# Adaptive-norm modulation in four column groups, token rows loaded between its units

## The chip, the cores and the metric

One Trainium2 chip, one core of it. The metric is the device time of one execution in microseconds (us); the kernel before takes 2986.76 us (median of three runs, 2984.95 to 2987.01). One execution was also recorded by the hardware profiler. The engines are named as in the profile: PE is the matrix engine, PEld its weight loads, DVE the vector engine, ACT the scalar engine, POOL the general engine, SP the engine whose queue issues nearly all DMAs.

## The reference, cut to what matters

Two blocks of two transformer layers, on 512 tokens of width 1024 and 256 context tokens. The first block modulates its norms by a condition vector:

```
def adaln(cond, w, b):
    m = jnp.matmul(jax.nn.silu(cond), w) + b
    return jnp.split(m, 3, axis=-1)
...
for layer in range(DEPTH):
    shift, scale, gate = adaln(c, w_ada[layer], b_ada[layer])
    c_shift, c_scale, c_gate = adaln(c_ctx, w_ada[layer], b_ada[layer])
    h = modulated_norm(x, norm_g[layer], shift[:, None], scale[:, None])
    h_ctx = modulated_norm(x_ctx, norm_g[layer], c_shift, c_scale)
    p = jnp.matmul(h, w_in[layer])
    ...
    x = x + gate[:, None] * jnp.matmul(y, w_out[layer])
```

`w_ada[layer]` is 1024 x 3072. Only two rows (c and c_ctx) are multiplied with it, so the work is loading 12.6 MB a layer and streaming it through PE. Layer 0 mixes tokens by global attention (GQA) and by a long convolution (the hyena branch), whose filters come from a small network and are used in the frequency domain. All outputs are f32.

## The kernel before, in words

Ordinary products run as three matmuls on f32 numbers split into a high and a low part (`mm3`, L81 to L83; splits at L54 and L55). The modulation does not: `ada` (L141 to L183) multiplies in f32 itself. It goes over chunks of 512 of the 3072 columns. A chunk has four units; a unit loads 512 KB of weights into a tile `st` (L151; the tag `st` has four buffers, which every other weight uses too) and does two f32 matmuls (L160) whose stationary operand is two columns of the condition (`c2`) and whose moving operand is 128 x 512 weights. Eight matmuls add up in rows 0 and 1 of one PSUM tile. ACT copies these two rows (L164). For chunks 0 to 3 (shift and scale) four small transposes turn them into columns, DVE adds the bias (L171), and after chunk 3 the per-channel factors modA and modB are made (L181, L182). For chunks 4 and 5 (gate) the two rows go to DRAM, `grow` (L175). `gate_tile` (L185) later loads a gate row spread over all partitions (L188), loads the bias spread in the same way (L193) and adds it on POOL (L195).

The stages of layer 0 are written as generators that yield a cost after each piece of work. `merge` and `mix` (L1681 to L1698) take two of them and always advance the one that has used the smaller share of its declared total. A list scheduler behind the program then reorders each engine's instructions within their dependencies. The stages, with the times at which they ran:

- A, 0 to 265 us: the filter network and filter transforms (`hy_mlp`, `hy_kernels`) merged with `inputs()`. `inputs()` does the 16 units of layer 0's chunks 0 to 3, then loads the 6 blocks of token rows (2 of context, 4 of x; L202, tag `oa`), normalises them (`rms`, L206 to L219: squares on ACT, factors and products on DVE), transposes and modulates them (`mod_T`, L222 to L241) and projects them for the hyena branch.
- 265 to 340 us: the projections of the attention.
- C, about 340 to 448 us: attention merged with gates 4 to 7 and the 16 units of layer 1's chunks 0 to 3.
- D, 448 to 535 us: gates 0 to 3, then layer 0's gate chunks 4 and 5 (8 units), merged with the context's convolution.
- E, 535 to 662 us: the long convolution of x merged with the context's output and layer 1's chunks 4 and 5 (8 units).

Of the kernel before, what the change touches and what calls it, by code (L numbers as in the profile page):

```python
# [15 lines left out]
P = 128  # L16
# [11 lines left out]
class Net:  # L28
# [109 lines left out]
        self.split(V[:, :, 0], V[:, :, 1], s)  # L138


    def ada(self, l, chunks, exact=True, tag='o'):  # L141

        nc, I = self.nc, self.I
        nr = 2 if exact else 4
        self.exact[l] = exact
        for c in chunks:
            ps = self.ps(tag)
            for kk in range(4):
                if exact:
                    w = self.t('st', [P, 1024])  # L150
                    nc.sync.dma_start(w, I[f'ada{l}'][c * 4 + kk])  # L151
                    w = [w]
                else:
                    st, w = self.t('st', [P, 1024]), [self.t('a', [P, 1024], R) for _ in range(2)]
                    nc.sync.dma_start(st, I[f'ada{l}'][c * 4 + kk])
                    self.split(w[0], w[1], st)
                cc = self.c2 if exact else self.c4
                for j in range(2):
                    for x, v in enumerate(w):
                        nc.tensor.matmul(ps[:nr], cc[:, 2 * kk + j], v[:, j * 512:(j + 1) * 512],  # L160
                                         start=kk + j + x == 0, stop=2 * kk + j == 7 and x == len(w) - 1)
                yield 1.7 if exact else .85
            row = self.t('v2', [P, 512])
            nc.scalar.activation(row[:nr], ps[:nr], AF.Copy)  # L164
            if c < 4:
                pT = self.ps('pt')
                for b in range(4):
                    self.tr(pT[:, b * nr:(b + 1) * nr], row[:nr, b * P:(b + 1) * P], nr)
                pv = pT[:, :4 * nr].rearrange("p (m j) -> p m j", j=nr)
                d = self.adaT[l][:, c * 4:c * 4 + 4]  # L170
                nc.vector.tensor_tensor(d, pv[:, :, 0:2], self.adabT[l][:, c * 4:c * 4 + 4], op=OP.add)  # L171
                if not exact:
                    nc.vector.tensor_tensor(d, pv[:, :, 2:4], d, op=OP.add)
            else:
                nc.sync.dma_start(self.grow[l][0:nr, (c - 4) * 512:(c - 3) * 512], row[:nr])  # L175
            if c == 3:
                self.mod[l] = []
                for j in range(2):
                    a = self.cn.tile([P, 8], F, name=f"modA{l}_{j}")
                    b = self.cn.tile([P, 8], F, name=f"modB{l}_{j}")  # L180
                    nc.vector.scalar_tensor_tensor(a, self.adaT[l][:, 8:16, j], 1.0, self.ngc[l], op0=OP.add, op1=OP.mult)  # L181
                    nc.vector.tensor_copy(b, self.adaT[l][:, 0:8, j])  # L182
                    self.mod[l].append((a, b))  # L183

    def gate_tile(self, l, j):  # L185
        nc = self.nc
# [328 lines left out]
    def hy_taps(self, o, hf, ni, w3, C):  # L515
# [287 lines left out]
    def first_consts(self):  # L803
        nc, I = self.nc, self.I
        self.ones = self.cn.tile([P, P], F, name="ones")
        nc.gpsimd.memset(self.ones, 1.0)
        self.c2 = self.cn.tile([P, 8, 2], F, name="c2")
        cc = self.const('cT', I['cT'])
        nc.scalar.activation(self.c2, cc, AF.Tanh, scale=0.5)
        nc.vector.tensor_scalar(self.c2, self.c2, 0.5, 0.5, op0=OP.mult, op1=OP.add)  # L810
        nc.vector.tensor_tensor(self.c2, self.c2, cc, op=OP.mult)
        self.mod, self.exact = [None, None], [None, None]
        self.grow = [self.scratch(f"grow{l}", [4, 1024]) for l in range(2)]
        self.c4 = self.cn.tile([P, 8, 4], R, name="c4")
        self.split(self.c4[:, :, 0:2], self.c4[:, :, 2:4], self.c2)
        self.adaT = [self.cn.tile([P, 16, 2], F, name=f"adaT{l}") for l in range(2)]

    def more_consts(self):
# [6 lines left out]
    def layer0(self, each):  # L825
# [4 lines left out]
        Y = []  # L830

        def inputs():
            ada = self.ada(0, range(4), True)
            for _ in range(3):
                yield next(ada)
            self.more_consts()
            yield from ada
            xc, xs = self.load_rows(I['ctx'], 2, 'oa'), self.load_rows(I['x'], 4, 'oa')
            self.rms(xc)
            self.rms(xs)  # L840
            hc, hx = self.ctx_T(), self.new_T()
            H.extend((hc, hx))
            yield 1
# [20 lines left out]
        def att():  # L864
# [4 lines left out]
            for g in range(2):  # L869
                K = C['K'][g]  # L870
                for i in range(4):
# [6 lines left out]
        self.merge(att(), 82, self.chain(self.gates('w0', 18, st, (4, 5, 6, 7)), self.ada(1, range(4), True, 'mm')), 58)  # L878
        self.merge(self.chain(self.gates('w0', 18, st, (0, 1, 2, 3)), self.ada(0, (4, 5), True)), 31,
                   self.hyena(1, yc[2:]), 13)  # L880

        def ctx_out():
            y = self.y_split(yc, 256)
            xc = self.load_rows(I['ctx'], 2)
            yield from self.out_proj('wout0', y, 2, xc, self.gate_tile(0, 1), lambda i: None)
            del y
            self.hc1 = self.ctx_h(xc)
            yield 2
            yield from self.ada(1, range(4, 6), True)
# [1046 lines left out]
    def build(self, stage="all"):  # L1936
        tc, nc, I = self.tc, self.nc, self.I
        with ExitStack() as top:
# [14 lines left out]
            if first:  # L1953
                self.first_consts()
                hx = None
                if stage == 'l1':
                    self.xscr = I['x']
                    self.more_consts()
                    self.run(self.ada(1, range(6), False))
# [66 lines left out]
def constants():  # L2026
# [21 lines left out]
    for n in (512, 256):  # L2048
# [6 lines left out]
        for ix in tok[n]:  # L2055
            zf.append(z[ix])
            dec.append(d[ix])
    C['hyz'] = np.concatenate(zf, 0).T.astype(f32)
    C['hydec'] = np.stack(dec, 0).astype(f32)
    row0 = np.ones((P, 1), f32)  # L2060
    row0[0] = 0
# [154 lines left out]
```

## Time and profile before

| | |
|---|---|
| median of three runs | 2986.76 us |
| the profiled execution, its own time | 2990.1 us |
| its span, first to last instruction | 2988.3 us |
| PE busy | 2819.3 us, 94% |
| DVE busy | 1973.2 us, 66% |
| ACT busy | 1347.9 us, 45% |
| POOL busy | 266.8 us, 9% |
| mean granted PE clock | 0.98 |
| PE busy in the first 80 us | 61.6 us |

Busy time is a sum over stages with different limits, so each stage has to be read by itself: how much of it PE worked, and where PE did not, what it waited for. An f32 matmul shows as two records of PE, each with its own weight load. The name `oa`, `st` or `grow` in a row is that of the tile, and L160 is the line of the program that issued it.

### The profile page before, as it was taken

The numbers are of one execution on the slowest core, as the hardware profiler recorded it, in microseconds if no ns is written. First come the engines' busy times: TensorE is split into PE (matmuls) and PEld (weight loads), VectorE is DVE, ScalarE is ACT, GpSimd is POOL, SyncE is SP. The second block draws the span as 40 slices with busy tenths as digits, with TensorE's granted clock in tenths as the row PEclk, the third lists the DMA queues.
The fourth block names the chain that finished last, engine by engine and source line by source line (L and its number), as shares of the span: only waits on it lengthen the run. The fifth ranks groups of instructions, "written<-read, shape, count | busy, mean of one in ns | idle before, by whom it ended". The sixth has DMA issues, their size and how long they took to land.

```text
span 2988.3 us, 40380 instructions
## 1 busy us (share of the span) xinstructions
PE 2819.3 (94%) x14904; PEld 2286.7 (77%) x14904; DVE 1973.2 (66%) x4419; ACT 1347.9 (45%) x2763; POOL 266.8 (9%) x310
## 2 busy tenths in 40 slices
PE   7999899889899999999999899999999999899998
PEld 3788757557888778777788788888787778788886
DVE  5767867986787756876755843436787664954435
ACT  6543445343345644565543522324565552633222
POOL 0212101101211310100110000000000011000000
PEclk8999999989999999999999999999999999999999
DMA  6433132653213423221124132233231124223231
GB/s 225 136 123 97 36 106 85 218 183 104 76 54 112 123 84 99 95 70 61 55 85 148 65 120 90 95 106 123 66 98 58 57 71 148 85 85 112 93 98 64
DMA packets 117645, 299.76 MB, mean 100 GB/s; under 512 B 21471, under 2 KB 48031, under 8 KB 117448
## 3 DMA queue, kind: packets, MB, share of 16 engines
q1 hardware_dynamic: 117448, 297.19, 30.3%
q8 instruction: 117, 1.92, 0.3%
q14 instruction: 80, 0.66, 0.1%
HBM read 273.54 MB, written 27.54 MB: 101 GB/s over the span
## 4 chain that ended last, share of the span: by engine, by line
PE 60%; DVE 8%; ACT 3%; issue 1%; DMA 0%; POOL 0%; ACTq 0%; DVEq 0%
PE mm L81 15%; PE mm L82 15%; PE mm L83 15%; PE pt L86 4%; PE o L120 2%; PE o L121 1%; PE o L1026 1%; DVE u L55 1%; PE o L1437 1%; PE S L1632 1%; DVE a L1141 1%; PE S L1633 1%; PE o L1492 1%; DVE a L1137 0%; PE S L1402 0%
## 5 line engine op out<-in xcount | busy, mean ns | idle before, releaser
L81 PE MATMUL mm<-a,u 128*128 128x512 f32 (+1 forms) x1596 | 595.8, 375 | 6.5 <-ACT a L54 2.4
L82 PE MATMUL mm<-a,u 128*128 128x512 f32 (+1 forms) x1596 | 593.1, 372 | 0.0
L83 PE MATMUL mm<-a,u 128*128 128x512 f32 (+1 forms) x1596 | 588.9, 370 | 0.4 <-DVE u L55 0.4
L54 ACT ACTIVATE u<-st 128x1024 fp32r<-128x1024 f32 x352 | 368.7, 1051 | 409.6 <-PE mm L83 355.1
L55 DVE TENSOR_TENSOR u<-st,u 128x1024 fp32r<-128x1024 f32 x340 | 427.9, 1259 | 130.6 <-ACT u L54 124.2
L81 PE MATMUL mm<-u,a 128*128 128x512 f32 (+1 forms) x1280 | 459.7, 360 | 10.8 <-DVE v L259 3.7
L82 PE MATMUL mm<-u,a 128*128 128x512 f32 (+1 forms) x1280 | 458.1, 358 | 4.6 <-DVE u L55 4.6
L83 PE MATMUL mm<-u,a 128*128 128x512 f32 (+1 forms) x1280 | 458.3, 358 | 0.0
L81 PEld LDWEIGHTS mm<-a,u 128*128 128x128 f32 x1596 | 302.2, 190 | 57.6 <-ACT a L54 4.3
L83 PEld LDWEIGHTS mm<-a,u 128*128 128x128 f32 x1596 | 302.6, 190 | 47.3 <-DVE u L55 1.0
L82 PEld LDWEIGHTS mm<-a,u 128*128 128x128 f32 x1596 | 303.0, 190 | 44.4 <-issue 1.5
L81 PEld LDWEIGHTS mm<-u,a 128*128 128x128 f32 x1280 | 243.0, 190 | 48.0 <-ACT u L54 3.7
L82 PEld LDWEIGHTS mm<-u,a 128*128 128x128 f32 x1280 | 243.4, 190 | 39.6 <-DVE u L55 6.8
L83 PEld LDWEIGHTS mm<-u,a 128*128 128x128 f32 x1280 | 243.2, 190 | 34.6 <-DVE a L58 0.6
L86 PE MATMUL pt<-c_ident,e 128*128 128x128 f32 x1132 | 191.1, 279 | 37.6 <-DVE e L273 9.4
L55 DVE TENSOR_TENSOR va<-pt,va 128x512 fp32r<-128x512 f32 (+2 forms) x252 | 163.6, 668 | 72.4 <-ACT va L54 71.3
L54 ACT ACTIVATE va<-pt 128x512 fp32r<-128x512 f32 (+2 forms) x252 | 140.7, 582 | 155.8 <-PE pt L86 153.0
L1206 DVE SCALAR_TENSOR_TENSOR a<-a,mm 128x512 f32<-128x512 f32 x96 | 65.7, 684 | 213.1 <-PE mm L83 213.0
L86 PEld LDWEIGHTS pt<-c_ident,e 128*128 128x128 f32 x1132 | 135.7, 141 | 82.4 <-issue 34.8
L1891 DVE TENSOR_TENSOR v<-v 128x512 f32<-128x512 f32 x64 | 44.3, 692 | 157.4 <-ACT v L1890 157.4
L1890 ACT ACTIVATE v<-mm 128x512 f32<-128x512 f32 x60 | 36.0, 600 | 200.3 <-PE mm L83 200.3
L82 PE MATMUL S<-u,a 128*128 128x256 f32 x312 | 90.1, 289 | 1.4 <-DVE u L55 1.4
(425 smaller groups left out, 4948.1 us busy)
## 6 DMA issues: line engine op xcount, KB each, us to landing
st<-in_up SPq DMA_DIRECT2D x64, 512.0 KB
st<-in_dn SPq DMA_DIRECT2D x64, 512.0 KB
st<-in_w SPq DMA_DIRECT2D x52, 512.0 KB
st<-in_ada SPq DMA_DIRECT2D x48, 512.0 KB
st<-in_gate SPq DMA_DIRECT2D x48, 512.0 KB
st<-in_win SPq DMA_DIRECT2D x42, 512.0 KB
st<-in_wout SPq DMA_DIRECT2D x24, 512.0 KB
st<-in_br SPq DMA_DIRECT2D x16, 512.0 KB
```

What stands on the lines that cost most here:

```text
L54: nc.scalar.activation(hi, src, AF.Copy)
L55: (eng or nc.vector).tensor_tensor(lo, src, hi.bitcast(F), op=OP.subtract)
L81: mm(ps, ah, bh, start=first, stop=False)
L82: mm(ps, ah, bl, start=False, stop=False)
L83: mm(ps, al, bh, start=False, stop=last)
L86: self.nc.tensor.transpose(dst, src, self.ident[:n, :n])
L120: nc.tensor.matmul(o, v, ph[:nk], start=first and bi == 0, stop=False)
L121: nc.tensor.matmul(o, v, pl[:nk], start=False, stop=last and bi == len(blocks) - 1)
L1026: nc.tensor.matmul(o[s * 64:(s + 1) * 64, i * P:(i + 1) * P], v[:, hd * 64:(hd + 1) * 64], pe[:, b * P:(b + 1) * P], start=b == 0, stop=b ...
L1206: self.nc.vector.scalar_tensor_tensor(xx, xx, alpha, ps, op0=OP.mult, op1=OP.add, **kw)
L1890: nc.scalar.activation(r, ps, AF.Relu)
L1891: nc.vector.tensor_tensor(sq, r, r, op=OP.mult)
```

## The change

- `ada`: the stationary operand is 32 columns wide, two of the condition and zeros behind them (`cw`), and the eight matmuls of a chunk go to four groups of 32 output partitions in turn, so neighbours write different columns of the array. Each group adds up two of the eight. ACT copies all 128 rows. For chunks 0 to 3 four f32 matmuls with a constant (`asel`) sum the groups and turn them into columns in one step. For chunks 4 and 5 the bias row is loaded into row 2 of the copy (2 KB), one f32 matmul with `asel` sums groups and bias, ACT copies two rows, and these go to `grow`.
- `gate_tile` is one load; the bias loads and the POOL adds are gone.
- The declared costs: a unit yields 0.5 where it yielded 1.7, and 3.0 inside `inputs()`.
- `inputs()` loads the token rows behind unit 3 of 16 and normalises them behind units 4 and 5; the declared total of that stream goes from 135 to 156.
- `hy_taps` takes its tiles from the tag `oa` in one case, (o, hf) = (0, 1), and from `u` in the others.

```diff
-    def ada(self, l, chunks, exact=True, tag='o'):
+    def ada(self, l, chunks, tag='o', pace=0.5):
...
                 for j in range(2):
-                    for x, v in enumerate(w):
-                        nc.tensor.matmul(ps[:nr], cc[:, 2 * kk + j], v[:, j * 512:(j + 1) * 512],
-                                         start=kk + j + x == 0, stop=2 * kk + j == 7 and x == len(w) - 1)
-                yield 1.7 if exact else .85
+                    k = 2 * kk + j
+                    g = slice(32 * (k % 4), 32 * (k % 4) + 32)
+                    nc.tensor.matmul(ps[g], self.cw[:, 2 * k:2 * k + 32], w[:, j * 512:(j + 1) * 512], start=k < 4, stop=k >= 4)
+                yield pace
             row = self.t('v2', [P, 512])
-            nc.scalar.activation(row[:nr], ps[:nr], AF.Copy)
+            nc.scalar.activation(row, ps, AF.Copy)
             if c < 4:
                 pT = self.ps('pt')
                 for b in range(4):
-                    self.tr(pT[:, b * nr:(b + 1) * nr], row[:nr, b * P:(b + 1) * P], nr)
+                    nc.tensor.matmul(pT[:, 2 * b:2 * b + 2], row[:, b * P:(b + 1) * P], self.asel[:, 0:2],
+                                     start=True, stop=True)
...
             else:
-                nc.sync.dma_start(self.grow[l][0:nr, (c - 4) * 512:(c - 3) * 512], row[:nr])
+                nc.sync.dma_start(row[2:3], I[f'adab{l}'][0:1, c * 512:(c + 1) * 512])
+                pg = self.ps('pt')
+                nc.tensor.matmul(pg[:2], self.asel[:, 2:4], row, start=True, stop=True)
+                gr = self.t('v2', [P, 512])
+                nc.scalar.activation(gr[:2], pg[:2], AF.Copy)
+                nc.sync.dma_start(self.grow[l][:, (c - 4) * 512:(c - 3) * 512], gr[:2])
...
         g = self.t('a', [P, 1024])
-        nc.sync.dma_start(g, rowb(self.grow[l], 1024, j * 1024))
-        low = [] if self.exact[l] else [(self.grow[l], (j + 2) * 1024)]
-        for src, off in low + [(self.I[f'adab{l}'], 2048)]:
-            for c in range(2):
-                b = self.t('v2', [P, 512])
-                nc.sync.dma_start(b, rowb(src, 512, off + c * 512))
-                sl = slice(c * 512, (c + 1) * 512)
-                nc.gpsimd.tensor_tensor(g[:, sl], g[:, sl], b, op=OP.add)
+        self.nc.sync.dma_start(g, rowb(self.grow[l], 1024, j * 1024))
         return g
...
-        if ni == 0 and hf == 0:
+        if ni == 0 and (o, hf) == (0, 1):
             E = [self.t('oa', [P, 2, 2, 256], R) for _ in range(nb)]
...
-            ada = self.ada(0, range(4), True)
+            ada = self.ada(0, range(4), pace=3.0)
             for _ in range(3):
                 yield next(ada)
             self.more_consts()
+            xc, xs = self.load_rows(I['ctx'], 2, 'oa'), self.load_rows(I['x'], 4, 'oa')
+            for _ in range(1):
+                yield next(ada)
+            self.rms(xc)
+            yield next(ada)
+            self.rms(xs)
             yield from ada
-            xc, xs = self.load_rows(I['ctx'], 2, 'oa'), self.load_rows(I['x'], 4, 'oa')
-            self.rms(xc)
-            self.rms(xs)
...
-        self.merge(self.chain(self.hy_mlp(), self.hy_kernels(1), self.hy_kernels(0)), 115, inputs(), 135)
+        self.merge(self.chain(self.hy_mlp(), self.hy_kernels(1), self.hy_kernels(0)), 115, inputs(), 156)
```

What this does to the order of instructions, at three places.

SP's queue in stage A, before: `in_ada` is the modulation's weights, `in_dft` and `in_hyw` belong to the filters, `in_ctx` and `in_x` are the token rows. These are the last units of chunks 0 to 3.

```order
L202 DMA oa_372<-in_ctx 128x1024
L506 DMA st_292<-in_dft 128x1024
L151 DMA st_307<-in_ada 128x1024
L151 DMA st_311<-in_ada 128x1024
L494 DMA st_315<-in_hyw 64x1024 x2
L151 DMA st_328<-in_ada 128x1024
L151 DMA st_332<-in_ada 128x1024
L202 DMA oa_374<-in_ctx 128x1024
L202 DMA oa_376<-in_x 128x1024
```

The same queue in the change, right behind the constants, at the fourth unit:

```order
L44 DMA c_hyc<-in_hyc 128x48
L194 DMA oa_174<-in_ctx 128x1024
L194 DMA oa_176<-in_ctx 128x1024
L194 DMA oa_178<-in_x 128x1024
L194 DMA oa_180<-in_x 128x1024
L194 DMA oa_182<-in_x 128x1024
L194 DMA oa_184<-in_x 128x1024
L152 DMA st_186<-in_ada 128x1024
```

All six row blocks (3.1 MB) now stand ahead of units 4 to 16; before, five of the six stood behind the last unit.

PE in stage C, before, where layer 1's first chunk starts (`mm_4130` is the modulation's PSUM tile, S and o the attention's):

```order
L83 MATMUL mm_3970<-a_455,u_3938 128x256
L160 MATMUL mm_4130<-st_4131,c_71 2x512
L404 MATMUL S_3813<-a_2313,a_2670 128x512
L405 MATMUL S_3813<-a_2313,a_2670 128x512
L404 MATMUL S_3818<-a_2313,a_2670 128x512
L405 MATMUL S_3818<-a_2313,a_2670 128x512
L160 MATMUL mm_4130<-st_4131,c_71 2x512
```

The same place in the change:

```order
L83 MATMUL mm_3968<-a_552,u_3936 128x256
L156 MATMUL mm_4128<-st_4129,cw 32x512
L385 MATMUL S_3805<-a_2313,a_2668 128x256 x4
L156 MATMUL mm_4128<-st_4129,cw 32x512
L156 MATMUL mm_4128<-st_4133,cw 32x512 x2
L156 MATMUL mm_4128<-st_4137,cw 32x512
L396 MATMUL S_3811<-a_2311,a_2668 128x512
L397 MATMUL S_3811<-a_2311,a_2668 128x512
```

The modulation's matmuls were mostly alone between others and now stand in longer runs.

SP at the end of stage E in the change (L170 loads a bias row into the copied rows, L175 stores the gate row, `in_wout` is the output weight); before, L175 stood there twice with no load ahead of it:

```order
L152 DMA st_5962<-in_ada 128x1024
L170 DMA v_1187_5867<-in_adab 1x512
L1174 DMA st_6138<-in_wout 128x1024
L1174 DMA st_6143<-in_wout 128x1024
L1174 DMA st_6148<-in_wout 128x1024
L175 DMA grow_81<-v_1189_5872 2x512
L170 DMA v_1215_5966<-in_adab 1x512
```

And PE there (L172 sums groups and bias, the S matmuls belong to the long convolution):

```order
L156 MATMUL o_5875<-st_5962,cw 32x512 x2
L172 MATMUL pt_5870<-v_1187_5867,c_asel 2x512
L172 MATMUL pt_5969<-v_1215_5966,c_asel 2x512
L81 MATMUL S_5945<-a_5562,a_5722 128x512
L82 MATMUL S_5945<-a_5563,a_5722 128x512
L83 MATMUL S_5945<-a_5562,a_5723 128x512
```

The second L172 has to wait for a load that stands behind the store of the first one's result.

## Rows read from the trace of the kernel before

**Rows 1.** The page: busy time, share of the span and instructions of each engine
```profile
PE 2819.3 (94%) x14904; PEld 2286.7 (77%) x14904; DVE 1973.2 (66%) x4419; ACT 1347.9 (45%) x2763; POOL 266.8 (9%) x310
```

**Rows 2.** Busy time by stretch; columns in the first line
```profile
core 0: us, PE busy (x) PEld busy (x) DVE busy (x) ACT busy (x) POOL busy (x), PEclk, DMA share, GB/s
0.00:54.00 54.00, 47.03 (x152) 16.17 (x152) 26.30 (x59) 24.80 (x44) 3.23 (x8) 0.97 0.80 259
54.00:80.00 26.00, 14.60 (x61) 10.86 (x60) 21.22 (x62) 24.85 (x55) 0.82 (x1) 0.67 0.32 110
80.00:265.00 185.00, 171.93 (x1079) 154.63 (x1079) 129.94 (x189) 87.63 (x139) 39.59 (x26) 0.97 0.39 123
...
387.00:448.00 61.00, 61.00 (x231) 25.88 (x230) 38.67 (x93) 29.88 (x79) 0.73 (x1) 1.00 0.42 129
448.00:535.00 87.00, 83.28 (x432) 59.81 (x432) 70.50 (x139) 43.44 (x99) 10.29 (x8) 1.00 0.28 89
535.00:662.00 127.00, 101.66 (x389) 65.62 (x388) 116.64 (x169) 50.59 (x79) 11.16 (x6) 0.90 0.59 204
```

**Rows 3.** PE timeline, 53 to 61 us: start, us, work [idle before, releaser]
```profile
53.49 0.64 PE L541 MATMUL S<-a,v 128*128 128x256 f32 x4
60.85 2.20 PE L86 MATMUL pt<-c_ident,oa 128*128 128x128 f32 x8 [6.72 <-DVE oa L219]
```

**Rows 4.** Line L214 (rms): count, duration in ns min/median/max, first and last start
```profile
L214 ACT ACTIVATE v<-oa x12: 612/613/614, 51.6 to 61.8; 128x512 f32<-128x512 f32 x12
L214 ACT ACTIVATION_READ_ACCUMULATOR v<-oa x12: 184/186/187, 52.1 to 62.3; 128x1 f32 x12
```

**Rows 5.** Line L160, the modulation's records on PE, same columns
```profile
L160 PE MATMUL o<-st,c x128: 589/592/1057, 8.1 to 652.7; 128*2 128x512 f32 x128
...
L160 PE MATMUL mm<-st,c x64: 591/592/593, 387.6 to 447.4; 128*2 128x512 f32 x64
```

**Rows 6.** PE timeline around a run and around a single f32 matmul
```profile
35.59 3.60 PE L160 MATMUL o<-st,c 128*2 128x512 f32 x8
...
387.30 0.28 PE L82 MATMUL mm<-a,u 128*128 128x256 f32 x1
387.42 0.28 PE L83 MATMUL mm<-a,u 128*128 128x256 f32 x1
387.63 1.02 PE L160 MATMUL mm<-st,c 128*2 128x512 f32 x2
388.58 0.50 PE L404 MATMUL S<-a,a 128*128 128x512 f32 x1
388.92 0.40 PE L405 MATMUL S<-a,a 128*128 128x512 f32 x1
389.15 0.40 PE L404 MATMUL S<-a,a 128*128 128x512 f32 x1
```

**Rows 7.** PE timeline: the four small transposes, and 32 matmuls with 64 moving columns
```profile
18.05 0.41 PE L86 MATMUL pt<-c_ident,v 2*128 2x2 f32 x4
...
1235.96 3.76 PE L1492 MATMUL o<-a,st 128*128 128x64 f32 x32 [0.31 <-issue]
```

**Rows 8.** SP timeline: the modulation's loads, the token rows, a small load
```profile
0.74 0.40 SPq L44 DMA_DIRECT2D c_cT<-in_cT  x1
...
17.15 13.32 SPq L151 DMA_DIRECT2D st<-in_ada  x6
...
45.02 1.93 SPq L202 DMA_DIRECT2D oa<-in_x  x4
```

**Rows 9.** ACT: the small load's reader, and the copies of line L164
```profile
2.37 0.21 ACT L809 ACTIVATE c<-c_cT 128x16 f32<-128x16 f32 x1 [0.35 <-DMA c_cT<-in_cT]
...
L164 ACT ACTIVATE v<-o x8: 573/587/591, 17.2 to 653.3; 2x512 f32<-2x512 f32 x8
```

**Rows 10.** PE timeline at the end of stage E
```profile
636.86 3.60 PE L160 MATMUL o<-st,c 128*2 128x512 f32 x8
...
647.47 0.40 PE L81 MATMUL S<-a,a 128*128 128x512 f32 x1
```

**Rows 11.** Line L195, the gate's bias adds on POOL
```profile
L195 POOL TENSOR_TENSOR a<-a,v x6: 1267/1484/2341, 574.6 to 1085.1; 128x512 f32<-128x512 f32 x6
```

More of the change, by code (lines that the diff above doesn't have):

```diff
@@ L138, in vsplit @@
         self.split(V[:, :, 0], V[:, :, 1], s)
-    def ada(self, l, chunks, exact=True, tag='o'):
+    def ada(self, l, chunks, tag='o', pace=0.5):
         nc, I = self.nc, self.I
-        nr = 2 if exact else 4
-        self.exact[l] = exact
         for c in chunks:
@@ L148, in ada @@
             for kk in range(4):
[L149 to L157, printed above, removed]
+                w = self.t('st', [P, 1024])
+                nc.sync.dma_start(w, I[f'ada{l}'][c * 4 + kk])
                 for j in range(2):
-                    for x, v in enumerate(w):
-                        nc.tensor.matmul(ps[:nr], cc[:, 2 * kk + j], v[:, j * 512:(j + 1) * 512],
-                                         start=kk + j + x == 0, stop=2 * kk + j == 7 and x == len(w) - 1)
-                yield 1.7 if exact else .85
+                    k = 2 * kk + j
+                    g = slice(32 * (k % 4), 32 * (k % 4) + 32)
+                    nc.tensor.matmul(ps[g], self.cw[:, 2 * k:2 * k + 32], w[:, j * 512:(j + 1) * 512], start=k < 4, stop=k >= 4)
+                yield pace
             row = self.t('v2', [P, 512])
-            nc.scalar.activation(row[:nr], ps[:nr], AF.Copy)
+            nc.scalar.activation(row, ps, AF.Copy)
             if c < 4:
@@ L167, in ada @@
                 for b in range(4):
[L168 to L169 removed]
+                    nc.tensor.matmul(pT[:, 2 * b:2 * b + 2], row[:, b * P:(b + 1) * P], self.asel[:, 0:2],
+                                     start=True, stop=True)
                 d = self.adaT[l][:, c * 4:c * 4 + 4]
[L171 to L175 removed]
+                nc.vector.tensor_tensor(d, pT[:, :8].rearrange("p (m j) -> p m j", j=2),
+                                        self.adabT[l][:, c * 4:c * 4 + 4], op=OP.add)
+            else:
+                nc.sync.dma_start(row[2:3], I[f'adab{l}'][0:1, c * 512:(c + 1) * 512])
[4 more added lines that the diff above has]
+                nc.sync.dma_start(self.grow[l][:, (c - 4) * 512:(c - 3) * 512], gr[:2])
             if c == 3:
@@ L806, in first_consts @@
         nc.gpsimd.memset(self.ones, 1.0)
-        self.c2 = self.cn.tile([P, 8, 2], F, name="c2")
+        self.cw = self.cn.tile([P, 46], F, name="cw")
+        nc.gpsimd.memset(self.cw, 0.0)
+        c2 = self.cw[:, :16].rearrange("p (k j) -> p k j", j=2)
         cc = self.const('cT', I['cT'])
[L809 to L815, printed above, removed]
+        self.asel = self.const('asel', I['asel'])
+        nc.scalar.activation(c2, cc, AF.Tanh, scale=0.5)
+        nc.vector.tensor_scalar(c2, c2, 0.5, 0.5, op0=OP.mult, op1=OP.add)
+        nc.vector.tensor_tensor(c2, c2, cc, op=OP.mult)
+        self.mod = [None, None]
+        self.grow = [self.scratch(f"grow{l}", [2, 1024]) for l in range(2)]
         self.adaT = [self.cn.tile([P, 16, 2], F, name=f"adaT{l}") for l in range(2)]
@@ L877, in layer0 @@
         self.run(self.gqa_proj('w0', ((hc, 2, 1, True), (hx, 4, 0, True)), gain, C))
-        self.merge(att(), 82, self.chain(self.gates('w0', 18, st, (4, 5, 6, 7)), self.ada(1, range(4), True, 'mm')), 58)
-        self.merge(self.chain(self.gates('w0', 18, st, (0, 1, 2, 3)), self.ada(0, (4, 5), True)), 31,
+        self.merge(att(), 82, self.chain(self.gates('w0', 18, st, (4, 5, 6, 7)), self.ada(1, range(4), 'mm')), 58)
+        self.merge(self.chain(self.gates('w0', 18, st, (0, 1, 2, 3)), self.ada(0, (4, 5))), 31,
                    self.hyena(1, yc[2:]), 13)
@@ L888, in ctx_out @@
             yield 2
-            yield from self.ada(1, range(4, 6), True)
+            yield from self.ada(1, range(4, 6))
         self.merge(self.hyena(0, yx[2:]), 49, ctx_out(), 48)
@@ L1958, in build @@
                     self.more_consts()
-                    self.run(self.ada(1, range(6), False))
+                    self.run(self.ada(1, range(6)))
                     self.hc1 = self.ctx_h(self.load_rows(I['ctx0'], 2))
@@ L2058, in constants @@
     C['hyz'] = np.concatenate(zf, 0).T.astype(f32)
+    sel = np.zeros((P, 4), f32)
+    for j in range(2):
+        sel[j::32, j] = 1
+        sel[j::32, 2 + j] = 1
+    sel[2, 2:] = 1
+    C['asel'] = sel
     C['hydec'] = np.stack(dec, 0).astype(f32)
```

1 line of the change is left out of this document (removed).

## The prediction
> **What bounds the kernel now.** I read the page's engine table first: PE works 94% of the span, nothing else over 66% [rows 1]. So time comes from PE, either as work taken off it or as holes filled. Then the busy times by stretch, for the stages that the change touches [rows 2]. The reader is to see four different stages. In the first 54 us PE works 47.03, and the DMA engines 0.80 of the time at 259 GB/s. From 54 to 80 us PE works only 14.60 of 26. Stage C has PE at 61.00 of 61 us and stage D at 83.28 of 87: PE sets their lengths. In stage E DVE works 116.64 of 127 us and PE 101.66: there DVE leads. Third, PE's timeline at the hole behind 54 us [rows 3]: PE stands 6.72 us until DVE has normalised the first token rows, so `rms` is last there. Line L214 shows why [rows 4]: its 12 squares, 0.613 + 0.186 us each, 9.6 us in all, start at 51.6 us, when the modulation is done. Last, the modulation's own records [rows 5, 6].
>
> **What a modulation matmul costs.** There are 128 + 64 records [rows 5] for 96 matmuls, two each, 64 matmuls and 128 records outside stage C. A run of 8 records takes 3.60 us, the last one 0.59: (3.60 - 0.59)/7 = 0.43 us apart [rows 6], 0.86 us a matmul. Around a single one the starts are farther apart: 0.21 us into it where its neighbours are 0.12 apart, 0.95 us for itself, and 0.34 behind it where 0.23 is usual [rows 6]. That is 0.09 + 0.09 + 0.11, about 0.28 us for every run of them, whatever its length.
>
> The order counts 26 runs in stage C before and 15 after (lengths 1, 4, 3, 1, 1, 2, 1, 4, 3, 2, 2, 2, 2, 1, 3), 7 before and 5 after in D (8, 1, 3, 2, 2).
>
> **How far column groups overlap** is what the sum hangs on, and no row of this trace has matmuls in different column groups side by side. Bounds: nothing overlaps (0.86 each, runs alone get fewer), or four always run as one. I take the value between. A matmul is two records into the same columns, so the second must follow the first, 0.43 us later, as now. In every row read here PE starts records in program order. So, if groups overlap, the second record of one can run beside the first of the next, and a run of n takes (n + 1) x 0.43 + 0.28 us.
>
> The Trainium skill (TensorEngine Tiling (Array Packing), Theoretical Speedup) gives up to four times for 32 columns and says that tiles work independently (Key Properties). By it the sum below would be that of the first rival. The page TensorE: Matmul & The Clock Gate, Part 3, has three column groups measured at 2.38 times, and says that matmuls start and end in program order; the latter, applied to two records a matmul, leads to my middle value. No row here shows either.
>
> **The change, part by part.**
>
> *Stage A.* Rows and `rms` leave the tail. First, what it can win: the hole of 6.72 us [rows 3], plus the waits that ACT's 9.6 us of squares [rows 4] put into the modulating chain; PE has 11.4 us of holes from 54 to 80 [rows 2]. Second, what it can lose: the rows' 3.1 MB now stand ahead of 13 of 16 units on SP. Up to 54 us 14.0 MB come in (259 x 54); at the same share-to-rate ratio full use would be 259/0.80 = 324 GB/s, 43 us for the same bytes. So the rows fit into capacity that was idle, and the last unit stays near 51 us. Were they not to fit, 3.1 MB at 259 GB/s is 12 us, of which the hole's 6.72 are paid back: a loss of 5. PE's own modulation there shortens as well, but shorter than its weights' arrival it can't get. I take -8, the hole and little more, since the rest of the chain (ACT and DVE 24.85 and 21.22 of 26 us busy [rows 2]) stays. Bounds -16 and +5. The `oa`/`u` exchange and `cw` have one answer, nothing: buffers, with PE's other work beside them.
>
> *Stage C.* 32 matmuls. Before: 64 records x 0.43 + 26 x 0.28 = 34.8 us. After: (32 + 15) x 0.43 + 15 x 0.28 = 24.4. That is -10.4, all on the path, as PE is full. Added: the four sums of L163 are f32 too, 8 records with full-width weights; 32 matmuls that are short on the moving side take 3.76 us, 0.12 each [rows 7], so 0.94 a chunk against 0.41 for the four transposes: +0.5 x 4 chunks. Stage C: -8.3. Bounds: -15.6 (15 groups of 0.86 + 0.28 = 17.1) and -1.0 (64 x 0.43 + 15 x 0.28 = 31.7).
>
> *Stage D.* 16 matmuls: 32 x 0.43 + 7 x 0.28 = 15.7 before, 21 x 0.43 + 5 x 0.28 = 10.4 after, -5.3. Two L172 are added at 0.86 + 0.28 = 1.14: +2.3. Stage D: -3.0; bounds -6.8 (six groups of 0.86, the run of eight being two, and 5 x 0.28) and +1.7 (32 x 0.43 + 5 x 0.28).
>
> *Stage E.* DVE sets it, so PE's saving there counts only at the end, where the six S matmuls start 10.6 us after the modulation's first long run [rows 10]. Now: eight matmuls (9 x 0.43 + 0.28 = 4.1), L172 (1.14), ACT's copy (0.59 [rows 9]), the store's issue (0.40) and the bias row's load. A small load was issued at 0.74 and held ACT until 2.37 us: 1.6 [rows 8, 9]. Then the second L172: 9.0 us together. I take 0; bounds -2 and +5.
>
> *Cover.* The modulation was PE's filler between the dependent steps of attention. With 10 us less of it I allow +2 for waits that come out, of ACT for PE first (bounds 0 and +5).
>
> *Nothing else.* The 128-row copy has as many elements per row as the 2-row one (0.59 [rows 9]). The POOL adds (1.3 to 2.3 us [rows 11]) and bias loads end long before the output projection reads the gate, with POOL at 9% [rows 1]; the matmuls of that projection hide them. Without that cover they would be worth under 5 us.
>
> **The sum:** -8 - 8.3 - 3.0 + 0 + 2 = -17.3 us. The profiled execution took 2990.1 us, so 2972.8; it lies 3.3 above the median of 2986.76, which gives **2969.5 us** for the median.
>
> **Rivals.**
>
> *Four groups run as one.* For it: the outputs are different columns, weights load beside running matmuls (PEld [rows 2]). Against: two records a matmul, in order. -8 - 15.6 - 6.8 + 2 = -28.4: 2958 us.
>
> *The groups do not overlap.* Then the change does not do what it says. For it: the records in the trace stand 0.43 us apart, one behind the other, and no row shows two outputs side by side. -8 - 1.0 + 1.7 + 2 = -5.3: 2981.5 us; if stage A gains less, no change.
>
> *Slower: SP's queue holds the gate matmuls up.* L172 waits on PE for a bias row that L170 loads, in a queue that serves in order. At the end of E the second L170 stands behind three loads of `in_wout`, which need free `st` buffers, and behind the store of the first gate row, which needs the first L172. All S matmuls behind L172 wait with it. Six loads through these buffers have taken 13.32 us [rows 8], 2.2 each; three are 6.7 us a place. With all four L172 held so, 27 us: -17.3 + 27 = +9.7, about 2996.5 us. It decides from 23 us of such waits (17.3, and 6 to be seen). For it: the order. Against: in D there is other work ahead of L172, and in E DVE lags anyway.
>
> **How the numbers follow.** Chances: my forecast 0.38, four as one 0.28, no overlap 0.21, the queue 0.13. The range reaches from a little below the second (2954) to the upper bounds of the third (2988); it leaves out the queue's case and a tail below. A measurement of this kernel can tell about 0.2%, 6 us, from no change. Faster by more: 0.37 of the forecast, 0.28, and 0.08 of the third case, 0.73. Within: 0.13 of the third and 0.01 of the last, 0.14. Slower: 0.12 of the last and 0.01 of the forecast with its bad bounds, 0.13.
>
> **What would show it.** In the changed profile PE's first token transposes (L86 from `oa`) should start near 53 us and not 60.85, with DMA share over 0.9 before them. In C the modulation's records should start 0.43 us apart in pairs; four records together mean the first rival, none overlapping the second. C should end 6 to 10 us earlier relative to its start. At L172 PE should wait under 5 us; over 6 in several places is the queue. If E grows by more than 5 us, or the row loads push the last unit past 58 us, the prediction is wrong.

## The result, and the profile after

The change is slower: 3018.61 us (median of four runs, 3013.88 to 3019.58) against 2986.89 before, a ratio of 1.0096 (95% interval 1.0083 to 1.0109). The forecast was 2969.5, faster. The profiled execution of the change took 3013.88 us, the quickest of the four, with a span of 3012.1.

The page of the changed kernel, engine by engine, answers to [rows 1]:

```profile
PE 2794.6 (93%) x14944; PEld 2296.5 (76%) x14944; DVE 1970.4 (65%) x4418; ACT 1349.5 (45%) x2766; POOL 255.7 (8%) x305
```

PE is busy 24.7 us less, as intended, and the span is 23.8 us longer: 48 us of new waits. The medians differ by 31.7 us; the other 8 us lie between the two profiled executions and their medians, and no trace shows them. Where the waits lie is read from the same stretches of stage A as in [rows 2], of the changed kernel:

```profile
0.00:54.00 54.00, 30.69 (x123) 14.03 (x125) 32.82 (x87) 28.24 (x57) 3.54 (x9) 0.83 0.77 241
54.00:80.00 26.00, 19.75 (x116) 15.12 (x113) 15.35 (x33) 19.11 (x34) 3.20 (x3) 0.83 0.57 174
80.00:265.00 185.00, 159.49 (x944) 140.04 (x943) 112.53 (x168) 86.82 (x140) 30.33 (x20) 0.95 0.33 108
```

PE does 210 us of work in the first 265 where it did 234: the modulation's saving, and some 10 us of other work that now comes later. The hole of [rows 3] is smaller (19.75 us busy of 26 instead of 14.60), but the DMA engines, busy 0.80 of the time before, are no busier than 0.77 while more is asked of them, and the granted clock of PE is 0.83 where it was 0.97, a mean over times at 2.4 GHz and times at 1.2 GHz.

That 0.77 is a mean over unlike parts. From 15 to 22 us, first the kernel before, then the change:

```profile
15.00:22.00 7.00, 6.98 (x20) 1.36 (x18) 4.71 (x12) 2.54 (x5) 0.00 (x0) 1.00 0.94 263
```

```profile
15.00:22.00 7.00, 0.04 (x1) 0.00 (x0) 5.61 (x22) 4.86 (x13) 0.00 (x0) 0.74 1.00 392
```

Right behind the issue of the six row loads (9.2 to 12.4 us) the DMA engines are fully busy at 392 GB/s, and PE does next to nothing. From 30 to 40 us they are busy only 0.47 of the time, where before it was 0.83.

PE's timeline in the changed kernel (start, us, work, idle before and releaser) shows the packed matmuls, a wait for their weights, the new sums and the first token transposes:

```profile
22.43 1.92 PE L156 MATMUL o<-st,cw 128*32 128x512 f32 x4 [7.39 <-DMA st<-in_ada]
...
35.98 1.05 PE L156 MATMUL o<-st,cw 128*32 128x512 f32 x4
...
37.63 1.07 PE L156 MATMUL o<-st,cw 128*32 128x512 f32 x8
...
40.17 0.95 PE L163 MATMUL pt<-c_asel,v 128*128 128x2 f32 x8
...
64.96 0.64 PE L86 MATMUL pt<-c_ident,oa 128*128 128x128 f32 x4
```

Eight records, four matmuls, take 1.07 us; in [rows 6] eight took 3.60. So the column groups do run together, all four. But PE waited 7.39 us for weights until 22.43 us; the four records behind that wait took 1.92 us, the four at 35.98 us 1.05. A second wait of 4.44 us ends at 31.36 us: PE needs weights of the filters that DVE takes up only at 27.41 us, when they are loaded, and that ACT splits (L54) at 30.69 us, behind eight of the norm's squares, which now come early (L206). The first token transposes start at 64.96 us, where [rows 3] has 60.85.

The modulation's matmuls in the first 120 us, changed kernel (count, ns min/median/max, first and last start); before, the last started at 50.3:

```profile
L156 PE MATMUL o<-st,cw x64: 592/617/1064, 8.6 to 61.5; 128*32 128x512 f32 x64
```

The last place to look at is the first attention, which spans stages C and D. Line L121 multiplies its values, so its first and last start bracket it. First the kernel before, then the change:

```profile
L121 PE MATMUL o<-va,a x56: 387/396/504, 343.3 to 516.0; 128*128 128x512 f32 x56
```

```profile
L121 PE MATMUL o<-va,a x56: 389/397/506, 361.2 to 539.9; 128*128 128x512 f32 x56
```

The attention begins 17.9 us later and takes 178.7 us instead of 172.7. From its last matmul to the end of the span it is 2472.3 us before and 2472.2 after. **All of the loss that the two traces show lies ahead of the attention's end: 18 us before it starts and 6 within it.** Stage E and what follows it have, taken together, neither gained nor lost.

### The profile page after: what moved, and what is told of

The parts are those of the page before. It is cut to its first block, busy times and chain, and to the rows that moved or that the text cites. A ratio compares the mean times of both kernels' runs of the same rounds, so it can differ in the third digit from the quotient of the medians.

```text
span 3012.1 us, 40456 instructions
## 1 busy us (share of the span) xinstructions
PE 2794.6 (93%) x14944; PEld 2296.5 (76%) x14944; DVE 1970.4 (65%) x4418; ACT 1349.5 (45%) x2766; POOL 255.7 (8%) x305
## 4 chain that ended last, share of the span: by engine, by line
PE 59%; DVE 8%; ACT 3%; issue 1%; DMA 0%; POOL 0%; ACTq 0%; DVEq 0%; SPq 0%; POOLq 0%
PE mm L81 15%; PE mm L82 15%; PE mm L83 15%; PE pt L86 4%; PE o L120 1%; PE o L121 1%; PE o L1022 1%; DVE u L55 1%; PE S L1628 1%; PE o L1433 1%; PE S L1629 1%; DVE a L1137 1%; PE o L1488 0%; DVE a L1133 0%; PE S L1398 0%
## 5 line engine op out<-in xcount | busy, mean ns | idle before, releaser
L83 PE MATMUL mm<-a,u 128*128 128x512 f32 (+1 forms) x1596 | 591.1, 371 | 1.6 <-DVE u L55 1.6
L54 ACT ACTIVATE u<-st 128x1024 fp32r<-128x1024 f32 x352 | 368.7, 1051 | 402.2 <-PE mm L83 355.8
L83 PE MATMUL mm<-u,a 128*128 128x512 f32 (+1 forms) x1280 | 458.5, 358 | 0.0
L83 PEld LDWEIGHTS mm<-a,u 128*128 128x128 f32 x1596 | 303.5, 190 | 48.3 <-DVE u L55 1.8
L83 PEld LDWEIGHTS mm<-u,a 128*128 128x128 f32 x1280 | 243.3, 190 | 34.8 <-DVE a L58 0.9
L86 PE MATMUL pt<-c_ident,e 128*128 128x128 f32 x1132 | 191.9, 280 | 34.7 <-DVE e L265 7.6
L54 ACT ACTIVATE va<-pt 128x512 fp32r<-128x512 f32 (+2 forms) x252 | 140.5, 582 | 163.6 <-PE pt L86 159.5
L86 PEld LDWEIGHTS pt<-c_ident,e 128*128 128x128 f32 x1132 | 136.2, 142 | 76.4 <-issue 27.7
L81 PE MATMUL S<-u,a 128*128 128x256 f32 x328 | 96.7, 296 | 7.4 <-DVE va L536 4.0
```

The costliest lines, as they stand in the source:

```text
L54: nc.scalar.activation(hi, src, AF.Copy)
L81: mm(ps, ah, bh, start=first, stop=False)
L83: mm(ps, al, bh, start=False, stop=last)
L86: self.nc.tensor.transpose(dst, src, self.ident[:n, :n])
```

## The experiments

The ratio to the kernel before is taken with runs on the same chip; on the chips of the experiments that kernel took 2988.7 to 2990.5 us. The table gives, from each profiled execution, the last unit of stage A, the first and last L121, and what is left of the span behind the last L121. These columns come from one execution each, and each edit also changes the order in which the list scheduler places the work, so a few us in them mean little.

| kernel | median us | ratio (95% interval) | last unit | L121 first, last | rest |
|---|---|---|---|---|---|
| before | 2986.9 | | 50.3 | 343.3, 516.0 | 2472.3 |
| the change | 3018.6 | 1.0096 (1.0083, 1.0109) | 61.5 | 361.2, 539.9 | 2472.2 |
| e1 | 2995.3 | 1.0015 (1.0005, 1.0024) | 50.3 | 346.8, 521.1 | 2473.6 |
| e2 | 2998.1 | 1.0030 (1.0017, 1.0044) | 50.6 | 347.6, 525.6 | 2469.2 |
| e3 | 3013.8 | 1.0087 (1.0072, 1.0102) | 62.5 | 363.9, 539.1 | 2473.5 |
| e4 | 3010.1 | 1.0076 (1.0060, 1.0092) | 61.9 | 361.8, 539.7 | 2467.9 |
| e5 | 2998.8 | 1.0027 (1.0016, 1.0037) | 50.0 | 347.6, 525.0 | 2473.0 |
| e6 | 3010.9 | 1.0066 (1.0050, 1.0083) | 61.6 | 362.7, 538.0 | 2470.3 |
| e7 | 3015.6 | 1.0082 (1.0067, 1.0097) | 64.2 | 367.2, 542.5 | 2470.8 |
| e8 | 2986.3 | 0.9989 (0.9979, 0.9999) | 51.0 | 344.3, 514.7 | 2471.0 |
| e9 | 3015.1 | 1.0098 (1.0075, 1.0122) | 55.1 | 363.3, 540.2 | 2473.5 |
| e10 | 2988.8 | 1.0002 (0.9992, 1.0012) | 48.9 | 341.1, 513.7 | 2468.7 |
| e11 | 3019.3 | 1.0104 (1.0080, 1.0129) | 63.3 | 364.0, 546.5 | 2472.8 |
| e12 | 2998.9 | 1.0037 (1.0025, 1.0049) | 49.4 | 346.1, 523.2 | 2477.0 |
| e13 | 2982.1 | 0.9977 (0.9967, 0.9987) | 51.7 | 342.0, 492.7 | 2487.5 |
| e14 | 2957.8 | 0.9896 (0.9875, 0.9918) | 52.0 | 348.4, 491.3 | 2466.5 |
| e15 | 2982.7 | 0.9979 (0.9968, 0.9990) | 50.4 | 342.8, 505.1 | 2475.5 |
| e16 | 2984.2 | 0.9984 (0.9973, 0.9995) | 48.8 | 344.9, 506.7 | 2471.7 |
| e17 | 2991.6 | 1.0005 (0.9996, 1.0015) | 51.4 | 342.6, 518.9 | 2467.6 |
| e18 | 2973.3 | 0.9949 (0.9937, 0.9961) | 51.9 | 342.1, 505.6 | 2466.6 |

### e1 to e4: the change taken apart

e1 is the change with this edit and a unit at 1.7 everywhere, and the tile tags of before; e2 has the same edit and tags and leaves 0.5 outside stage A.

```diff
-            ada = self.ada(0, range(4), pace=3.0)
+            ada = self.ada(0, range(4), pace=1.7)
             for _ in range(3):
                 yield next(ada)
             self.more_consts()
+            yield from ada
             xc, xs = self.load_rows(I['ctx'], 2, 'oa'), self.load_rows(I['x'], 4, 'oa')
-            for _ in range(1):
-                yield next(ada)
             self.rms(xc)
-            yield next(ada)
             self.rms(xs)
-            yield from ada
...
-self.merge(..., inputs(), 156)
+self.merge(..., inputs(), 135)
```

> The four column groups and the new gate path alone: token rows loaded and normalised after the last unit, 1.7 declared for a unit, total 135, and the tile tags of the filter sums as in the kernel before. Theory (the loss lies in the rows that come early and in the dealing, the packing itself gains): stage A ends no later than before (within 4 us of 265), the modulation's matmuls in stage C show four at a time, 1.05 us for a pair, and the time is 2968 to 2980. Rival (the packed matmuls or the new gate path lose the time): 2995 or more, with the late point in stages C to E. Second rival (packing is off the path, hidden): 2984 to 2990.

> The change with the token rows loaded and normalised after the last unit and the tags of the filter sums as before; a unit declared at 1.7 in stage A and at 0.5 elsewhere, as in the change, totals 135 and 58. Theory (two losses, of which only the first, in stage A, is undone): stage A ends near 265 us, the last weighted-value matmul of the first attention still comes late, and the time is 2990 to 3003, above the kernel with packing alone by 5 us or more. Rival (stage A is the whole loss): within 4 us of the kernel with packing alone.

e1 missed its theory of a gain and lies at the lower end of its first rival: with the rows late, packing does not lose what the change loses, but it does not gain either, 1.0015. e2 is 1.0030; the attention takes 178.0 us there and 174.3 in e1, but the two times are 3 us apart, as its rival said, and within the intervals. Both are far below the change: **the early rows and what goes with them are the larger loss.**

e3 and e4 are the change with one number altered:

```diff
-    def ada(self, l, chunks, tag='o', pace=0.5):
+    def ada(self, l, chunks, tag='o', pace=1.7):
```

```diff
-self.merge(att(), 82, ... self.ada(1, range(4), 'mm')), 58)
+self.merge(att(), 82, ... self.ada(1, range(4), 'mm')), 39)
```

> The change with one number put back: a unit declares 1.7 again outside stage A. Theory (the dealing of stage C delays the attention's end, behind which SP's queue is held): the queue's wait ends 5 to 12 us earlier and the time is 3006 to 3014 against 3018.6. Rival (the dealing of stage C is of no account, the delay comes whole from stage A): 3016 to 3021.

> The change with one number altered: the declared total of gates and modulation beside the attention is 39 and not 58, so that what is declared fits what is yielded (31 for the gates, 16 units of 0.5). The attention comes earlier in PE's order (its last matmul is number 2265 and not 2339). Theory (SP's queue is held until the attention's last tile is free, and stage E follows it): the queue's wait ends some 10 to 20 us earlier and the time is 2998 to 3010. Rival (stage E's start is set by other work): 3015 to 3021, though the attention ends earlier.

The medians moved 5 and 8 us the expected way (3 and 6 by the ratios), but the intervals of both reach into that of the change, so the dealing outside stage A, that is the order in which `merge` takes work from its two streams, is worth little or nothing that these runs can show. In e4 the attention was dealt earlier and yet its last matmul comes at 539.7 us: my picture of the loads in SP's queue did not hold, which e10 to e12 then tried directly.

### e5, e6, e7 and e9: which part of the early rows

e5 is e2 with the tile tags of the change. e6 is the change with 1.7 and 135 in stage A. e7 is e6 with 1.7 elsewhere as well and the rows loaded behind unit 12. e9 is e6 with the norm behind the last unit:

```diff
             xc, xs = self.load_rows(I['ctx'], 2, 'oa'), self.load_rows(I['x'], 4, 'oa')
-            for _ in range(1):
-                yield next(ada)
-            self.rms(xc)
-            yield next(ada)
-            self.rms(xs)
             yield from ada
+            self.rms(xc)
+            self.rms(xs)
```

> The kernel e2 (rows late, a unit at 1.7 in stage A and 0.5 elsewhere) with the tile tags of the filter sums as in the change. Theory (the rows' early place makes the loss of stage A, the tags do nothing): within 4 us of e2, 2994 to 3002, and the last filter matmul within 3 us of that of e2 (245 us). Rival (the tags cost, since the filter sums now share the tag u with split weights): 3004 or more, with the last filter matmul after 250 us.

> The change with the rows early, but a unit of stage A declared at 1.7 and the total 135 again. Theory (3.1 MB of rows ahead of 13 units make the modulation of stage A 11 us late, whatever is declared): last unit near 61 us, time 3012 to 3021. Rival (the declared 3.0 of 156 makes stage A late): 3000 or less.

> Packed modulation, 1.7 a unit, total 135, with the rows loaded behind unit 12 of 16 and normalised behind units 13 and 14, tags as in the change. Theory (only loads ahead of many units delay them; the hole before the first token transpose is real and can be closed): last unit at 50 to 55 us, first token transpose 5 us or more earlier than in e1 (63.6), time 2983 to 2992. Rival (any load ahead of units costs as much as the hole gives): 2995 to 3002.

> As e6 (rows loaded behind unit 3, 1.7 a unit, total 135), but normalised only after the last unit. Theory (the bytes of the rows in the DMA queues delay the units, the norm's own work does not): last unit after 58 us and 3005 to 3020. Rival (the squares and factors between the units hold up ACT and DVE, and with them the units): last unit near 51 us and 2990 to 3000.

The tags do nothing (e5, 2998.8 against 2998.1). The loads' place is the cause: e9 differs from e5 in nothing else and is 16 us slower, as slow as the change; e6, with the norm early as well, is 12 us slower than e5. e7, which was to be the good compromise, lies above both of its ranges: loads ahead of four units cost as much as loads ahead of thirteen, and the hole was not won at either place. The declared 3.0 of 156 may add something (e6 at 1.0066, the change at 1.0096; the intervals just touch).

How the 12 us arise is only half as expected. The last unit does come 11 us later in e6 (61.6 against 50.0), but only 5 later in e9 (55.1, where after 58 was expected), which loses more; so its lateness is not the loss. The first token transposes start at 63.8 us in e6 and 63.4 in e5, for there the norm is ready earlier. What is late in e6 is the filters' work, whose loads stand in the same queue: its first matmul of L527 starts at 36.7 us and not at 25.8, its first of L547 at 52.0 and not at 39.7. First e5, then e6, busy times from 82 to 140 us:

```profile
82.00:140.00 58.00, 50.49 (x292) 43.94 (x292) 36.21 (x55) 25.80 (x43) 9.21 (x6) 0.94 0.37 114
```

```profile
82.00:140.00 58.00, 46.43 (x236) 38.89 (x235) 28.06 (x45) 23.51 (x38) 7.03 (x4) 0.85 0.21 67
```

In e6 every engine works less there, DMA most of all (0.21 against 0.37), and PE at a lower granted clock. SP's timeline shows the first store of the filters (L580) and of the hyena inputs (L651), in e5:

```profile
84.58 1.27 SPq L580 DMA_DIRECT2D kscr<-va  x2
92.42 4.70 SPq L651 DMA_DIRECT2D z<-v  x2
```

and in e6:

```profile
91.55 3.13 SPq L651 DMA_DIRECT2D z<-v  x2
95.94 1.34 SPq L580 DMA_DIRECT2D kscr<-va  x2
```

The first L580 is 11 us late in e6, 15 in e9 (99.6) and 18 in e7 (102.8), and in all three it stands behind the first L651, where in e5, e1 and the kernel before it stands ahead. SP's longest wait in this stretch is no longer in e6 than in e5, only at another place (22.7 us at L651, 24.7 at L580). So moving the loads did two things: the loads behind them came later, and the scheduler placed the work in another order. No run parts the two, and which carries how much stays open. The change itself, with 3.0 of 156 declared, has a third order (its first L580 is at 64.4 us, its first L651 at 103.1), and only its total delay is like that of e6.

### e8: is PE the limit in stage C?

The kernel before, without 24 of the 32 modulation matmuls of stage C; it leaves out that part of the modulation's sum.

```diff
                 for j in range(2):
+                    if tag == 'mm' and 2 * kk + j not in (0, 7):
+                        continue
```

> The kernel before, with 24 of the 32 modulation matmuls of stage C left out (only the first and last of a chunk are done; loads, copies, transposes and all else stay). Theory (the attention's own chain sets stages C and D and the modulation only fills PE's waits): 2983 to 2994, within 4 us of before, PE idle in stage C where it had none. Rival, the reading of the prediction (PE is full, so work taken from it shortens the stage): 24 x 0.86 = 21 us and some runs less, 2962 to 2970.

Taking 21 us of work from an engine that was busy 61.00 of 61 us [rows 2] moved the time by 3 us (0.9989), and the attention by 2. Busy times over the attention (us, then PE, PEld, DVE, ACT, POOL, clock, DMA share, GB/s), before:

```profile
341.00:515.00 174.00, 172.50 (x861) 116.14 (x859) 126.89 (x292) 91.90 (x238) 11.83 (x11) 1.00 0.23 73
```

e8:

```profile
341.00:515.00 174.00, 159.89 (x821) 119.00 (x820) 128.79 (x295) 92.88 (x242) 11.62 (x12) 0.94 0.19 64
```

e1, with the matmuls packed, over its 175 us:

```profile
345.00:520.00 175.00, 162.72 (x873) 118.57 (x872) 126.75 (x293) 91.73 (x238) 11.65 (x12) 0.98 0.21 73
```

The attention nearly keeps its length and PE's saving turns into waits. Not all of it: PE is busy 12.6 us less in e8, not 21, at a granted clock of 0.94 where it was 1.00, so part of the saving went into slower matmuls (L86 takes 282 ns there in the mean, 275 before). How much of the kept length is the clock's was not tried by itself. PE's longest waits in e1 on the attention's other engines, over the same stretch; in the kernel before the largest is 0.5 us in total:

```profile
PE S L385 <- ACT e L413: 3.0, 3, 2.2
PE o L120 <- ACT va L54: 2.6, 5, 0.9
...
PE pt L86 <- DVE e L431: 2.0, 2, 1.1
```

These are steps of the attention, from engine to engine: scores, weighted values, transposes of the softmax's weights.

### e10, e11, e12: SP's queue

One edit, made to the kernel before, to the change and to e1:

```diff
-                    nc.sync.dma_start(p1, self.zscr[ctx][1][:, b])
+                    nc.gpsimd.dma_start(p1, self.zscr[ctx][1][:, b])
```

> The kernel before with one edit: the six small loads of the convolution's factors (tile va from DRAM scratch) are issued from POOL's queue and not from SP's. Theory (SP stands at the first of them for 48 us until the attention's last tile is free, and the loads of stage E wait behind it): SP's wait is gone, stage E starts earlier, and the time is 2970 to 2982. Rival (stage E starts when the attention ends for other reasons, SP's wait costs nothing): 2984 to 2992.

> The change with the same edit: those loads on POOL's queue. Theory (the 70 us wait on SP makes the hole of PE at 548 to 584 us): the holes of 4.4 and 10.5 us shrink to under 5 together and the time is 2995 to 3010. Rival: 3014 to 3021.

> e1 (packed modulation, rows late, 1.7 a unit) with the same edit. Theory (PE's time saved by packing becomes worth something once stage E's loads are not held): 2968 to 2982, below e10. Rival (the attention's own chain keeps the end where it is): equal to e10 within 4 us, or slower.

My theory fell in all three, and the rivals held: 1.0002, 1.0104, 1.0037. SP had stood 48.2 us at these loads before and 70.0 us in the change, and that looked like the cause. SP's timeline of e10 shows what took its place:

```profile
459.78 71.27 SPq L151 DMA_DIRECT2D st<-in_ada  x7
```

With the small loads gone from its head, the queue stands in the next ones, the gate chunks' weights, whose buffers come free only as PE gets to its modulation matmuls: from 440 to 560 us SP waits 64.6 us there for PE's L160. Here the queue follows PE and does not lead it.

### e13 to e16: the attention's chain

e13 is the kernel before and e14 is e1, each without the softmax's multiplications by the reciprocal sum in this attention, so that its weights are left undivided. e15 and e16 have the same two bases and leave nothing out: 44 of the 76 multiplications go to ACT, as in this diff.

```diff
                 e = ec[:, s * 256:(s + 1) * 256]
-                nc.vector.tensor_scalar(e, e, ri[:, s:s + 1], None, op0=OP.mult)
+                if self.plain:
+                    nc.scalar.activation(e, e, AF.Identity, scale=ri[:, s:s + 1])
+                else:
+                    nc.vector.tensor_scalar(e, e, ri[:, s:s + 1], None, op0=OP.mult)
```

> The kernel before, with the division by the softmax's sum left out in the first attention (76 DVE multiplications of 0.36 to 0.48 us on the way from the exponentials to the transposes, 31 us of DVE). Theory (the attention's own chain through DVE and ACT sets stages C and D, as long as PE's work or longer): if the chain is longer than PE's work, 2970 to 2980; if the two are equally long, PE is now the limit and nothing is won, 2984 to 2992. Rival (neither PE nor the chain but the loads or the order limit): 2984 to 2992 here and in the next too.

> e1 (packed modulation, rows late) with the same multiplications left out. Theory (chain and PE are equally long in the kernel before, so that only both together shorten the stage): the attention takes 165 us or less where it took 176 in e1, and the time is 2975 to 2987, 8 us or more below e1. Rival (something else, a load or the order of PE's queue, sets the attention's length): within 4 us of e1.

> The kernel before, with 44 of those multiplications (the context columns, 128x256) on ACT and not on DVE: the same result, DVE 15 us less in the attention, ACT some 20 more. Theory: PE is full in the attention, so no gain, 2984 to 2994. Rival (DVE alone is the limit): 2975 to 2982.

> e1 with 44 of the multiplications on ACT. Theory (the chain's length in sequence counts, not DVE's load, and ACT's step is no shorter): within 4 us of e1, 2990 to 3000. Rival (DVE's load is the limit once PE has room): 2980 to 2988.

Alone, the shorter chain gives 0.9977, 7 us: the attention ends 23 us earlier, but PE still has gates to do (48 of their L83 matmuls start within 60 us behind its last L121, where 9 did) and the rest behind it grows to 2487.5 us. Alone, packing gives 1.0015. Both together give 0.9896, some 35 us below e1 by the two ratios and below the range expected. That is the pattern of two limits of about equal length, the chain being the longer one by a few us, since only shortening it gave something by itself. e14's busy times over its attention:

```profile
348.00:491.00 143.00, 138.92 (x779) 101.37 (x778) 99.05 (x209) 89.71 (x230) 8.13 (x8) 1.00 0.26 90
```

PE is again nearly full, now in 143 us, and its clock is at 1.00. e15 and e16 point to DVE's load as a good part of the chain: 15 us moved to ACT gave 0.9979 and 0.9984, against my expectation that nothing would come of either.

### e17 and e18: only what pays

e17 is the kernel before with column groups in stage C alone; stage A and the gate path stay as they were. e18 adds the edit of e15.

```diff
-self.merge(att(), 82, ... self.ada(1, range(4), True, 'mm')), 58)
+self.merge(att(), 82, ... self.ada4(1, range(4), 'mm')), 58)
```

> The kernel before with column groups in stage C alone (layer 1's chunks 0 to 3); stage A, the gate chunks and the gate path as before. Theory (packing gains nothing beside a chain as long as PE's work; the 5 us by which e1 is above before come from stage A and the gate path): 2984 to 2990, no change. Rival (packing itself costs in stage C): 2991 or more.

> The same, with 44 of the softmax's multiplications on ACT as in e15. Theory (PE and the chain are both shortened, and nothing else of the change is there to cost): 2970 to 2980, below before, e15 and e16. Rival (only one of the two can be had): 2981 to 2985, as e15.

e17 is no change (1.0005), though its median of 2991.6 lies just above the expected range. **e18 takes 2973.3 us, 0.9949 (0.9937 to 0.9961), 16 us below the kernel before and, by the ratios, some 44 below the change**. e15 alone gave 6 us and e17 alone none.

## Why the prediction was wrong

- **"PE sets their lengths", stages C and D (-8.3 and -3.0).** This is the step that failed. PE was busy 61.00 of 61 us [rows 2], but with filler, work placed between the attention's dependent steps: an attention chain of about the same length ran beside it. e8 shows that PE's work alone is worth 3 us, e13 and e14 that both limits must go. The prediction's sentence on cover, that waits of 2 us would come out, had the right mechanism but not the size: the waits and the slower clock behind them took the whole of the saving, and the attention even took 6 us longer (178.7 against 172.7; 175 to 183 in the variants e3, e4, e6, e7, e9 and e11).
- **"So the rows fit into capacity that was idle", stage A (-8).** The second failure, and the one that made the sign. The last unit started at 61.5 us, not near 51 and past the 58 that the prediction named as its sign of being wrong: 11 us late, where the unfavourable bound said 12. Capacity was not what lacked: the reckoning gave 324 GB/s for full use, and 392 were reached from 15 to 22 us. But a mean over 54 us does not say when there is room: the rows stood first in the queue, PE waited 7.39 us for the weights behind them, and the room left later was not used. The early norm had a part that the sum did not have, through ACT: the last unit starts at 61.6 us in e6, and at 55.1 in e9, where the norm is late. The bound's price of +5 was far too low as well: it paid 6.72 us back for the hole and counted the modulation alone, while the filters' work, fed by the same queue, can become late too, as in e6. The attention starts 17.9 us later, of which e6 against e5 puts 15.1 on the early rows (362.7 against 347.6). How this splits between late loads and the other order of the work stays open.
- **The size of the miss.** The measured median lies 49 us above the forecast: some 26 from stage A (17.9 where -8 was forecast), some 15 from stages C and D with their cover (6 where -9.3 was), and the 8 that no trace shows.
- **How far groups overlap.** The middle value was wrong, the first rival right on this point: four matmuls in 1.07 us. The Trainium skill (TensorE: Matmul & The Clock Gate, Part 3) has tiles start some 4 ns apart; here the first records of four matmuls start at 37.626, 37.633, 37.640 and 37.646 us, and their second records from 38.081 on, 6 to 7 ns apart. My mistake was to let the second record of a matmul go ahead of the first of the next. With PE's saving worth nothing by itself, it made no difference to the time that these runs show.
- **L163 and L172.** Four sums take 0.95 us, as worked out (0.94). At the end of E, PE waited for the bias row as the order said:

```profile
669.21 1.87 PE L172 MATMUL pt<-v,c_asel 128*2 128x512 f32 x2 [4.37 <-DMA v<-in_adab]
```

  4.4 us, in one place. The forecast for stage E was 0, and the rest behind the attention is unchanged as a whole, so no loss shows there.
- **The slower rival.** Its sign was right and its mechanism was not: not the gate matmuls behind SP's queue (4.4 us at L172 for its bias row in all, where 23 were needed), but loads in stage A, which the prediction had as a bound and not as a rival.

## What to carry to other kernels

A full engine is a limit only if nothing else runs beside it for as long: before costing work taken from it, look whether the work it would leave behind is filler between the steps of another engine's chain, or leave that work out and see whether the time moves. A mean DMA share (0.80 over 54 us here) does not say that loads can be moved ahead for nothing: ask which loads stand behind them in the queue, of every stream that it feeds, and what waits for those. Two limits of about equal length show little or no gain for either alone (7 us in e13, none in e17) and a larger one together (some 31 us in e14, 16 in e18 against 6 in e15).

## What was not expected of the hardware

Four f32 matmuls in four column groups, two records each, ran in 1.07 us against 3.60 in one group, 3.4 times, and two in 1.05: a pair costs as much as four. The records of one matmul are not adjacent in start: in the run of four at 37.63 us all first records come before any second one. DMA share stayed at 0.77 over the first 54 us of the change, at 241 GB/s, although 13 units and six blocks of rows were asked for; from 15 to 22 us it was 1.00 at 392 GB/s, and up to 22.43 us PE waited 7.39 us for one unit's weights.
